# An encoder block on one core: filter spectra stored twice in DRAM, decay tiles loaded three ahead, the last hyena block loaded ahead

## The chip, the cores and the metric

The kernel runs on one core of one Trainium2 chip. The metric is the device time of one execution in microseconds (us). A core has TensorE (PE, matrix products and transposes through the systolic array into PSUM), VectorE (DVE), ScalarE (ACT) and GpSimd (POOL); SyncE (SP) issues nearly all the DMA transfers, which 16 DMA engines carry out.

## The reference, cut to what matters

One layer of a bidirectional encoder block, all in fp32, on 2048 positions and a model width of 1024. The projection to 2048 columns gives 512 columns for a Fourier mixing and 3 x 512 for a gated long convolution (hyena) of order two, whose filters are made by a small network and a decay.

```python
def implicit_filters(...):
    ...
    h = (h @ w_out).reshape(l, HYENA_ORDER, N_DIRECTIONS, HYENA_WIDTH)
    decay = jnp.exp(-t[:, None] * jnp.abs(deltas)[None, :])
    h = h * decay[:, None, None, :]
    ...
    return k * lax.rsqrt(jnp.sum(k * k, axis=0, keepdims=True) + EPS)

def fft_long_conv(u, k_freq, d):
    uf = jnp.fft.rfft(u, n=2 * l, axis=1)
    y = jnp.fft.irfft(uf * k_freq[None], n=2 * l, axis=1)[:, :l]
    return y + u * d

def hyena_mix(...):
    ...
    k_freq = jnp.fft.rfft(k, axis=0)
    z = v
    for n, gate in enumerate((x1, x2)):
        z = gate * fft_long_conv(z, k_freq[:, n], long_d[n])
    return z

def reference(...):
    h = rmsnorm(x, g_mix)
    p = h @ w_in                       # 512 Fourier columns, 3 x 512 hyena columns
    y_f = rmsnorm(fourier_mix(u_f), g_fourier)
    y_h = rmsnorm(hyena_mix(u_h, ...), g_hyena)
    x = x + concat(y_f, y_h) @ w_out
    x = x + relu(rmsnorm(x, g_mlp) @ w_fc1) ** 2 @ w_fc2
    return rmsnorm(x, g_final)
```

## The kernel before

The times below are those of the profiled execution. The kernel goes through these stages:

- `project` (0 to 410 us): x times the input weights in two passes; beside it tables are loaded (`tables`, the list `got`) and fc2's weights are combined. The gates x1, x2 and v go to DRAM (`gates`).
- `fourier` beside the first two filter units (410 to 473 us). The main loop takes a step of each in turn.
- the filter spectra (473 to 627 us), in `filters`: eight units, two orders n by four column tiles ct of 128 channels. A unit is made in three parts of eight steps: `generate(q)` (PE L529 into `pk`, DVE L533 `kt` = pk times the decay tile `dec`, ACT L181 `kh`, the fp32r upper part, and on DVE or POOL L182 `kl`, the rest; L543/544 add up squares), `stage1(c)` (three products L189 to L191, and DVE's transpose L443 into `Gk`) and `stage2(q)` (PE L597, ACT L600 into `ks`, and at every second q the store to `kd` in DRAM, called `spec`, L602). While unit i goes through stage1 (steps 0 to 7) and stage2 (8 to 15), unit i + 2 is generated, at the steps that the list `GENERATE` gives for i. `normalise` scales by the norm, `skip` adds long_d, `LAST` places unit 7's stage1.
- `hyena` (627 to 840 us): eight blocks, again n by ct. For each: `first` (PE L691, DVE L443 into G), `second(q)` (PE L698 into `pz`; ACT L701/702 `zs`; DVE L704 `y` = pz times ks; POOL L705 zs times ks; L706 adds them into y), `inverse(q)` three steps later (`LAG`, PE L714 into `pv`, ACT L715), `turn` (DVE L443) and `gate` (PE L727, DVE L728). `spectrum(q)` brings a tile ks of 512 KB by two transfers of 64 partitions each (L677), in four buffers.
- the tail of hyena (840 to 878 us): the first two tokens' Fourier rows (`yf`, L801/803, their norm L827, their transpose `pt_y` L810), the weights of w_out (`ost`, L792, split at L184/185), the last gates, and the Fourier half of the product `po` for these tokens.
- `project_out`, fc1 and fc2 (878 us to the end).

The order of the work on each engine is the order in which the code is written; SP takes its transfers in order too, and waits at each for its buffer. The long_d rows (`dk8`) are loaded inside `filters` (L505), behind the project stage's stores. A decay tile is loaded when the generate that uses it is written (two buffers, L170):

```python
if q % 2 == 0:
    self.dec = load(fp, "dec", [P, 8, 128], A["decay"][self.ct][:, 4 * q : 4 * q + 8, :], 2)
```

The table `f2` serves both the filters and hyena's second stage, `a2` the inverse; a2 is loaded into a pool of its own (2 MB, issued at 592 us).

Of the kernel before, what the change touches and what calls it, by code (L numbers as in the profile page):

```python
# [10 lines left out]
F32 = mybir.dt.float32  # L11
# [15 lines left out]
def _tables():  # L27
# [56 lines left out]
    A2[:, 0, 0] *= 0.5  # L84
    T["f2"] = F2.reshape(128, 32, 128).astype(f32)
# [42 lines left out]
P = 128  # L128
# [6 lines left out]
def hybrid_block(ctx: ExitStack, tc: tile.TileContext, A, out):  # L135
# [9 lines left out]
    kd = [[scratch(f"spec{i}{n}", [P, 32, 128]) for n in range(2)] for i in range(4)]  # L145
# [350 lines left out]
    def filters(ctx, fp, gp, zp, zzs, norms, emb, wo, e1k, f2):  # L496
# [10 lines left out]
        nc.tensor.transpose(p[:, 0:8], rows, ident[0:8, 0:8])  # L507
        nc.scalar.copy(longd, p[:, 0:8])

        class Unit:  # L510
# [3 lines left out]
            def generate(self, q):  # L514
# [9 lines left out]
                if q % 2 == 0:  # L524
                    self.dec = load(fp, "dec", [P, 8, 128], A["decay"][self.ct][:, 4 * q : 4 * q + 8, :], 2)
# [13 lines left out]
                if q == 0:  # L539
                    nc.scalar.square(self.acc, k4)  # L540
                else:
                    sq = fp.tile([P, 4, 128], F32, tag="sqr", name="sqr")
                    nc.scalar.square(sq, k4)  # L543
                    nc.gpsimd.tensor_add(self.acc, self.acc, sq)
# [49 lines left out]
            def stage2(self, q):  # L594
# [9 lines left out]
        units = [Unit(ct, n) for n in range(2) for ct in range(4)]  # L604
        for u in units[:2]:
# [9 lines left out]
        GENERATE = [(3, 5, 7, 7, 9, 11, 13, 15)] * 5 + [(7, 7, 8, 9, 10, 11, 12, 13)]  # L615

        LAST = ((), (), (), (), (), (0, 1, 2), (3, 4, 5), (6, 7))
        for i, u in enumerate(units):
            new = units[i + 1] if i < 7 else None

            def generate(step):
                for q in range(8 if i < 6 else 0):
                    if GENERATE[i][q] == step:
                        units[i + 2].generate(q)

            for c in range(8 if new else 0):
# [3 lines left out]
                generate(c)  # L630
            for q in range(8):
                u.stage2(q)
                if i == 6:
                    for c in LAST[q]:
                        new.stage1(c)
                if i and new and q == (0 if i == 6 else 1):
                    new.normalise()

                if new and q == (2, 5, 5, 5, 5, 5, 4)[i]:
                    new.skip()  # L640
                generate(8 + q)
                if q % 4 == 0 and i > 4:
                    ct = 2 * i - 11 + q // 4
                    if 0 <= ct < 4:
                        cs = slice(128 * ct, 128 * ct + 128)
                        if ct == 0:
                            zzs.append(zp.tile([P, NT, 512], F32, tag="zz", name="zz"))
                        nc.sync.dma_start(zzs[0][:, :, cs], gd[0][:, :, cs])
                j = 8 * i + q - 50
                if 0 <= j < 8:  # L650
                    units[j // 2].scale(2 * (j % 2), nc.gpsimd)
                    units[j // 2].scale(2 * (j % 2) + 1, nc.vector)


    def hyena(hp, wp, rp, zz, e1, b1, f2, a2, out_weights, out_ahead):
# [6 lines left out]
        class Block:  # L662
            def __init__(self, n, ct):
                self.n, self.ct = n, ct
                self.cs = slice(128 * ct, 128 * ct + 128)
                self.y, self.ahead = {}, None
# [5 lines left out]
            def spectrum(self, q):  # L672

                ks = hp.tile([P, 2, 4, 128], F32, tag="ks", name="ks", bufs=4)
# [19 lines left out]
            def second(self, q):  # L694
                ks = self.ahead if q == 0 and self.ahead else self.spectrum(q)
# [737 lines left out]
```

## Time and profile before

| what | value |
|---|---|
| runs before | 2334.44, 2330.9, 2318.71 us |
| median | 2330.9 us |
| profiled execution | 2326.34 us |
| its span in the profile | 2324.5 us |
| mean granted clock of TensorE | 0.988 of full speed |

The rows further down are of four views. A row of the windows view gives a stretch of the span in us (from:to, then its length), for each engine its busy time and in brackets its instructions, then the share of TensorE's full clock that was granted (PEclk), the mean busy share of the DMA engines and what they moved. PEld are weight loads beside PE's products. A row of the timeline gives the start of an instruction, its time, engine, line, operation, output<-inputs, shapes and count, and in square brackets the idle time of the engine before it with what ended it. For SPq, the DMA-issuing queue of SP, it is the issue, not the transfer. A row of the groups by line gives the count, the busy time in us, the mean of one in ns, and the idle time before them with what ended it.

### The profile page before, as it was taken

Reading aid. Unit: us, or ns where it says so; the run is one execution under the profiler, and the core shown is the slowest. Engines: PE = TensorE matmul, PEld = TensorE weight load, DVE = VectorE, ACT = ScalarE, POOL = GpSimd, SP = SyncE. Lnnn points to the kernel's source line nnn. Section 1 sums busy time; section 2 is a strip of 40 time slices with the busy share of each in tenths; the row PEclk is TensorE's granted clock in tenths of the full one; section 3 lists DMA queues with packets and bytes.
Section 4 is the critical chain, followed back from the end, with each engine's and each line's share of the span. In section 5 each row is a group of like instructions: output and inputs, shape, how many; then the busy total and the mean of one; then the engine's idle time right before and its main releaser. Section 6 shows DMA issues by size and latency. Waiting matters only on the chain.

```text
span 2324.5 us, 31068 instructions
## 1 busy us (share of the span) xinstructions
PE 2244.5 (97%) x11025; PEld 1859.5 (80%) x11025; DVE 1514.7 (65%) x2256; ACT 1108.8 (48%) x1842; POOL 827.4 (36%) x625
## 2 busy tenths in 40 slices
PE   7999999899999979998999999999999999999998
PEld 6887788698888758886788877888888888888886
DVE  6999676677677775457544456444366666866667
ACT  6555211465455554445555556555543333533334
POOL 3444332567366532116655556555400000000000
PEclk9999999999999999999999999999999999999999
DMA  7535986557689985667544455444479766866631
GB/s 253 182 136 197 330 303 244 189 194 240 223 194 204 206 235 163 186 177 233 162 152 153 151 205 193 150 150 150 160 283 361 241 191 193 291 207 191 198 119 73
DMA packets 294716, 468.42 MB, mean 202 GB/s; under 512 B 18389, under 2 KB 142623, under 8 KB 290209
## 3 DMA queue, kind: packets, MB, share of 16 engines
q1 hardware_dynamic: 288897, 452.04, 61.3%
q10 hardware_dynamic: 5664, 14.41, 1.8%
q8 instruction: 86, 1.41, 0.3%
q14 instruction: 69, 0.57, 0.1%
HBM read 312.54 MB, written 152.27 MB: 200 GB/s over the span
## 4 chain that ended last, share of the span: by engine, by line
PE 62%; DMA 4%; DVE 4%; ACT 2%; issue 1%; POOL 1%; SPq 1%; POOLq 0%; DVEq 0%; ACTq 0%
PE p1u L189 5%; PE p1u L191 5%; PE p1u L190 5%; PE p2u L191 5%; PE p2u L189 5%; PE p2u L190 5%; PE p2v L189 3%; PE p2v L191 2%; PE p2v L190 2%; PE p1v L189 2%; PE p1v L191 2%; PE p1v L190 2%; DMA ks<-spec 2%; PE po L190 2%; PE po L191 2%; PE po L189 2%
## 5 line engine op out<-in xcount | busy, mean ns | idle before, releaser
L181 ACT CAST qahm<-ra 128x1024 fp32r<-128x1024 f32 x110 | 115.9, 1053 | 345.8 <-PE p2u L190 172.7
L182 DVE TENSOR_TENSOR qalm<-ra,qahm 128x1024 fp32r<-128x1024 f32 x110 | 134.6, 1224 | 154.6 <-ACT qahm L181 151.8
L1208 POOL TENSOR_TENSOR acc<-acc,gfin 128x512 f32<-128x512 f32 x4 | 5.1, 1277 | 633.0 <-DMA out<-acc 625.8
L189 PE MATMUL pu<-wh,xh 128*128 128x512 f32 x512 | 204.2, 400 | 5.8 <-ACT wh L184 4.6
L190 PE MATMUL pu<-wl,xh 128*128 128x512 f32 x512 | 201.1, 393 | 3.3 <-DVE wl L185 3.3
L191 PE MATMUL pu<-wh,xl 128*128 128x512 f32 x512 | 200.9, 393 | 1.7 <-DVE xl L182 1.6
L190 PE MATMUL p2u<-qblm,qahm 128*128 128x512 f32 x504 | 196.2, 389 | 0.5 <-DVE qblm L182 0.5
L189 PE MATMUL p2u<-qbhm,qahm 128*128 128x512 f32 x504 | 196.0, 389 | 0.0
L191 PE MATMUL p2u<-qbhm,qalm 128*128 128x512 f32 x504 | 195.8, 389 | 0.0
L182 DVE TENSOR_TENSOR qblm<-rb,qbhm 128x1024 fp32r<-128x1024 f32 x110 | 134.0, 1218 | 1.9 <-ACT qbhm L181 1.9
L380 POOL TENSOR_TENSOR acc<-acc,cw 128x512 f32<-128x512 f32 x45 | 59.4, 1320 | 201.5 <-DVE acc L357 200.0
L181 ACT CAST ahm<-s 128x512 fp32r<-128x512 f32 x124 | 76.6, 620 | 95.2 <-PE p1v L190 54.6
L182 POOL TENSOR_TENSOR alm<-W,ahm 128x512 fp32r<-128x512 f32 x63 | 85.3, 1354 | 92.9 <-ACT ahm L181 92.9
L189 PEld LDWEIGHTS pu<-wh,xh 128*128 128x128 f32 x512 | 97.1, 190 | 26.4 <-ACT wh L184 5.0
L181 ACT CAST qbhm<-rb 128x1024 fp32r<-128x1024 f32 x110 | 115.4, 1049 | 5.2 <-DMA a1m<-c 3.4
L190 PEld LDWEIGHTS pu<-wl,xh 128*128 128x128 f32 x512 | 97.1, 190 | 24.2 <-DVE wl L185 3.8
L191 PEld LDWEIGHTS pu<-wh,xl 128*128 128x128 f32 x512 | 97.0, 189 | 23.1 <-DVE xl L182 2.5
L190 PEld LDWEIGHTS p2u<-qblm,qahm 128*128 128x128 f32 x504 | 94.6, 188 | 20.6 <-DVE qblm L182 1.0
L189 PEld LDWEIGHTS p2u<-qbhm,qahm 128*128 128x128 f32 x504 | 94.5, 188 | 20.2 <-ACT qbhm L181 0.4
L191 PEld LDWEIGHTS p2u<-qbhm,qalm 128*128 128x128 f32 x504 | 94.6, 188 | 19.8
L189 PE MATMUL p1u<-bm,ahm 128*128 128x512 f32 x252 | 100.2, 398 | 7.2 <-ACT ku L1071 6.3
L181 ACT CAST ahm<-W 128x512 fp32r<-128x512 f32 x94 | 57.6, 615 | 102.5 <-PE p1u L190 96.0
(387 smaller groups left out, 6449.2 us busy)
## 6 DMA issues: line engine op xcount, KB each, us to landing
W<-in_w_fc SPq DMA_DIRECT2D x66, 512.0 KB, 4.6
ks<-spec SPq DMA_DIRECT2D x128, 256.0 KB, 6.6
rb<-td SPq DMA_DIRECT2D x64, 512.0 KB, 4.2
ra<-a1m SPq DMA_DIRECT2D x56, 512.0 KB, 6.8
ra<-a0m SPq DMA_DIRECT2D x54, 512.0 KB, 10.6
rb<-in_w_fc SPq DMA_DIRECT2D x46, 512.0 KB, 4.5
f<-in_w_fc SPq DMA_DIRECT2D x16, 1024.0 KB, 6.8
td<-f SPq DMA_DIRECT2D x16, 1024.0 KB, 5.2
```

The lines of the kernel that those rows point to most:

```text
L181: nc.scalar.copy(hi, src)
L182: (eng or nc.vector).tensor_sub(lo, src, hi)
L189: nc.tensor.matmul(o, lhsT=lh, rhs=rh, start=start, stop=False, skip_group_check=more)
L190: nc.tensor.matmul(o, lhsT=lh, rhs=rl, start=False, stop=False, skip_group_check=more)
L191: nc.tensor.matmul(o, lhsT=ll, rhs=rh, start=False, stop=stop, skip_group_check=more)
L380: nc.gpsimd.tensor_add(m1, m1, cw[:, 3, :])
L1208: nc.gpsimd.tensor_mul(acc[i][:, c], acc[i][:, c], gfin[:, c])
```

## The change

- The long_d rows (`dk8`) are loaded in the project stage, and emb's tile moves to the pool `tp`.
- `decay(k)` loads the decay tiles, from the third unit on three ahead of their use, in four places (two `dec`, two in the pool of the x rows). `sqr` has two buffers.
- Spectra lie in DRAM twice, in a layout [2, 64, 2, 4096]: each store writes 128 x 2 x 1024 floats, 1 MB instead of 512 KB. For that the filters use a table `f2k` with permuted columns; hyena's own `f2` is loaded later into emb's tile (`tabs`), and a2 into the place of the filters' table. A spectrum is read by one transfer of 128 partitions, 512 KB.
- Hyena begins with the first four spectra of block 0, each followed by a quarter of a2.
- Unit 7's generates have other steps, partly in unit 6's stage1; zz is loaded and scaled by two tables, `LOAD` and `SCALE`.
- In the last block all spectra are asked for at q = 1 (q from 4 on in the room of W), then the Fourier rows, the first w_out rows and the gate rows; the tail's order of weights, gates, turns and products is another, the norms of the first two tokens' hyena rows come earlier (`norms`), and the pairs' places alternate between G and V.

```diff
-    kd = [[scratch(f"spec{i}{n}", [P, 32, 128]) for n in range(2)] for i in range(4)]
+    kd = [[scratch(f"spec{i}{n}", [2, 64, 2, 32 * 128]) for n in range(2)] for i in range(4)]
...
-        rows = fp.tile([8, 128], F32, tag="dk8", name="dk8")
-        for n in range(2):
-            nc.sync.dma_start(rows[4 * n : 4 * n + 4, :], A["long_d"].rearrange("a (c n) j -> n (a c) j", n=2)[n])
...
-                    self.dec = load(fp, "dec", [P, 8, 128], A["decay"][self.ct][:, 4 * q : 4 * q + 8, :], 2)
+                    k = 4 * units.index(self) + q // 2
+                    for j in (range(8, 12) if k == 8 else (k + 3,) if k > 8 else (k,)):
+                        decay(j)
+                    self.dec = decs.pop(k)
...
-                    nc.sync.dma_start(kd[self.ct][self.n][:, 4 * q - 4 : 4 * q + 4, :], self.ks)
+                    dst = kd[self.ct][self.n].rearrange("h p s x -> (p s) h x")[:, :, 512 * q - 512 : 512 * q + 512]
+                    nc.sync.dma_start(dst, self.ks.rearrange("p (h f) c -> p h (f c)", h=1).broadcast_to([P, 2, 1024]))
...
+                decs[k] = pl.tile([P, 8, 128], F32, tag=tag, name="dec", bufs=2)
+                nc.sync.dma_start(decs[k], A["decay"][u.ct][:, q : q + 8, :])
...
-        GENERATE = [(3, 5, 7, 7, 9, 11, 13, 15)] * 5 + [(7, 7, 8, 9, 10, 11, 12, 13)]
+        GENERATE = [(3, 5, 7, 7, 9, 11, 13, 15)] * 5 + [(7, 9, 11, 13, 15, 16, 17, 18)]
...
-                src = kd[self.ct][self.n][:, 4 * q : 4 * q + 4, :].rearrange("(s p) f c -> p s f c", s=2)
-                for hf in (slice(0, 64), slice(64, 128)):
-                    nc.sync.dma_start(ks[hf], src)
+                if self is blocks[7] and q > 3:
+                    if q == 4:
+                        self.room = rp.tile([P, 4, 2, 4, 128], F32, tag="W", name="ks4")
+                    ks = self.room[:, q - 4]
+                else:
+                    ks = hp.tile([P, 2, 4, 128], F32, tag="ks", name="ks", bufs=4)
+                src = kd[self.ct][self.n].rearrange("h p s x -> (h p) s x")[:, :, 512 * q : 512 * q + 512]
+                nc.sync.dma_start(ks.rearrange("p s f c -> p s (f c)"), src)
...
-                (nc.gpsimd if self is not blocks[7] and q in (0, 1, 2, 3) else nc.vector).tensor_add(y, y, zs)
+                (nc.gpsimd if q in ((0, 1) if self is blocks[7] else (0, 1, 2, 3)) else nc.vector).tensor_add(y, y, zs)
...
+        for k in range(4):
+            blocks[0].ahead[k] = blocks[0].spectrum(k)
+            nc.sync.dma_start(a2[:, 8 * k : 8 * k + 8], A["a2"][:, 8 * k : 8 * k + 8])
...
+                if i == 7:
+                    if q == 1:
+                        cur.ahead.update((k, cur.spectrum(k)) for k in range(2, 8))
+                    elif q == 2:
+                        ahead = work.ahead(hp, cur.y[2][:, 0, 0:1])
+                        next(ahead)
+                    elif q == 5:
+                        for k in range(4):
+                            work.load(hp, k)
+                    elif q == 6:
+                        cur.load()
...
-        old.load()
         for q in range(8 - LAG, 8):
             old.inverse(q)
-        ahead = out_ahead(hp)
-        next(ahead)
+        for k in range(0, 2):
+            work.weights(hp, k)
         for q in range(4):
             older.gate(q)
-            old.turn(2 * q)
-            old.turn(2 * q + 1)
-        next(ahead, None)
-        for k in range(0, 4):
-            out_weights(hp, k)
-        for q in range(4):
+        for k in range(2, 4):
+            work.weights(hp, k)
+        next(ahead)
+        for c in range(8):
+            old.turn(c)
+        for q in (0, 2):
+            next(ahead)
             old.gate(q)
-        next(ahead, None)
+            old.gate(q + 1)
+            if q == 0:
+                work.norms(hp)
         for k in range(4, 8):
-            out_weights(hp, k)
+            work.weights(hp, k)
...
-                n = "G" if k < 4 else "V"
+                n = "GVGV"[k // 2]
...
+            got.append(cpool.tile([8, 128], F32, tag="dk8", name="dk8"))
+            for n in range(2):
+                nc.sync.dma_start(got[-1][4 * n : 4 * n + 4, :], A["long_d"].rearrange("a (c n) j -> n (a c) j", n=2)[n])
```

The order of the instructions changes at these places. DVE at the start of the Fourier stage; Gf are its transposes, kt and kl belong to the first filter unit. Before:

```order
L182 TENSOR_TENSOR e1l<-e1k,e1h 128x128
L443 STREAM_TRANSPOSE Gf<-pf_3612 128x8x2x32
L533 TENSOR_TENSOR kt<-pk,dec 128x512
L536 COPY k_3638<-kt 1x128
L182 TENSOR_TENSOR kl<-kt,kh 128x4x8x16
L443 STREAM_TRANSPOSE Gf<-pf_3643 128x8x2x32
L443 STREAM_TRANSPOSE Gf<-pf_3646 128x8x2x32
L533 TENSOR_TENSOR kt<-pk,dec 128x512
```

and with the change:

```order
L185 TENSOR_TENSOR e1l<-e1k,e1h 128x128
L446 STREAM_TRANSPOSE Gf<-pf_3615 128x8x2x32
L446 STREAM_TRANSPOSE Gf<-pf_3643 128x8x2x32
L446 STREAM_TRANSPOSE Gf<-pf_3646 128x8x2x32
L536 TENSOR_TENSOR kt<-pk,dec 128x512 x2
L539 COPY k_3638<-kt 1x128
L185 TENSOR_TENSOR kl<-kt,kh 128x4x8x16
```

All three transposes stand ahead of the first kt now, where one did.

PE from unit 5's last first-stage products to unit 6's; L529 and L532 are a generate of unit 7, L597 and L600 a second-stage step of unit 5, L189 to L194 first-stage products. Before:

```order
L529 MATMUL pk<-wo,emb 128x128 x8
L597 MATMUL pk_5291<-Gk,f_2586 128x128 x4
L529 MATMUL pk<-wo,emb 128x128 x4
L597 MATMUL pk_5312<-Gk,f_2586 128x128 x4
L553 MATMUL psum_k<-ones,acc 128x1
L529 MATMUL pk<-wo,emb 128x128 x4
L597 MATMUL pk_5349<-Gk,f_2586 128x128 x4
L529 MATMUL pk<-wo,emb 128x128 x4
L597 MATMUL pk_5370<-Gk,f_2586 128x128 x4
L529 MATMUL pk<-wo,emb 128x128 x4
L597 MATMUL pk_5389<-Gk,f_2586 128x128 x4
L529 MATMUL pk<-wo,emb 128x128 x4
```

and with the change, from the second stage's end into unit 6's first stage:

```order
L532 MATMUL pk<-wo,emb 128x128 x4
L600 MATMUL pk_5392<-Gk,f_2589 128x128 x4
L600 MATMUL pk_5399<-Gk,f_2589 128x128 x4
L532 MATMUL pk<-wo,emb 128x128 x4
L192 MATMUL pk_5419<-kh,e1h 128x512
L193 MATMUL pk_5419<-kl,e1h 128x512
L194 MATMUL pk_5419<-kh,e1l 128x512
L532 MATMUL pk<-wo,emb 128x128 x4
L192 MATMUL pk_5437<-kh,e1h 128x512
L193 MATMUL pk_5437<-kl,e1h 128x512
L194 MATMUL pk_5437<-kh,e1l 128x512
L532 MATMUL pk<-wo,emb 128x128 x4
```

A generate stood beside each second-stage step; now it stands beside every second one, and the last three beside first-stage products of unit 6.

SP at the end of hyena; spec_67 is the last block's spectrum, xg its gate rows, yf the Fourier rows, ost the rows of w_out. Before:

```order
L670 DMA xg<-gates_59 128x16x128
L677 DMA ks<-spec_67 64x2x512 x8
L670 DMA xg<-gates_59 128x16x128
L801 DMA yf<-yfd 64x2x256
L803 DMA yf<-yfd 64x2x256
L801 DMA yf<-yfd 64x2x256
L803 DMA yf<-yfd 64x2x256
L792 DMA ost<-in_w_out 128x1024 x8
```

and with the change:

```order
L704 DMA ks<-spec_67 128x2x512
L704 DMA ks<-spec_65 128x2x512
L704 DMA ks<-spec_67 128x2x512 x3
L834 DMA ost<-in_w_out 128x1024 x2
L704 DMA ks_7326<-spec_67 128x2x512 x4
L853 DMA yf<-yfd 64x2x256
L855 DMA yf<-yfd 64x2x256
L853 DMA yf<-yfd 64x2x256
L855 DMA yf<-yfd 64x2x256
L834 DMA ost<-in_w_out 128x1024 x2
L692 DMA xg<-gates_59 128x16x128
L834 DMA ost<-in_w_out 128x1024 x4
```

The Fourier rows, half of the w_out rows and the last gate rows moved ahead, among the last block's spectra or right behind them.

## Rows read from the trace of the kernel before

**Rows 1.** Windows by stage, 400 to 425 and 573 to 2324 us, all engines.

```profile
core 0: us, PE busy (x) PEld busy (x) DVE busy (x) ACT busy (x) POOL busy (x), PEclk, DMA share, GB/s
...
400.00:425.00 25.00, 16.53 (x66) 12.13 (x65) 13.07 (x20) 2.69 (x7) 5.63 (x5) 0.80 0.71 244
...
573.00:630.00 57.00, 50.88 (x346) 45.74 (x345) 39.03 (x66) 26.12 (x52) 26.70 (x20) 0.94 0.70 238
630.00:807.00 177.00, 170.65 (x1190) 148.93 (x1188) 134.35 (x208) 98.76 (x171) 107.18 (x95) 1.00 0.89 202
807.00:840.00 33.00, 25.38 (x178) 21.02 (x180) 21.91 (x34) 16.64 (x30) 14.50 (x13) 0.95 0.96 217
840.00:878.00 38.00, 31.90 (x130) 20.48 (x127) 28.34 (x62) 23.16 (x43) 10.10 (x8) 0.87 0.74 227
878.00:2324.00 1446.00, 1419.45 (x6304) 1167.00 (x6302) 852.76 (x1180) 688.04 (x1081) 411.10 (x285) 0.99 0.58 190
```

**Rows 2.** Windows, the five stretches with a granted clock of about one half.

```profile
418.60:423.20 4.60, 4.56 (x12) 3.06 (x13) 1.08 (x3) 1.49 (x5) 0.00 (x0) 0.50 0.69 242
602.50:607.70 5.20, 5.17 (x24) 5.17 (x25) 1.35 (x7) 1.27 (x3) 0.00 (x0) 0.50 0.00 0
833.00:836.60 3.60, 3.08 (x15) 2.71 (x13) 2.33 (x5) 0.60 (x1) 2.54 (x3) 0.53 1.19 245
846.60:853.50 6.90, 6.29 (x18) 2.65 (x20) 6.90 (x12) 5.20 (x8) 0.00 (x0) 0.51 0.31 106
874.00:877.20 3.20, 3.20 (x11) 2.62 (x10) 1.38 (x2) 0.79 (x2) 0.83 (x1) 0.50 0.31 82
```

**Rows 3.** Timeline of PE at the start of the Fourier stage.

```profile
418.64 0.24 PE L507 MATMUL plongd<-ident,dk 8*128 8x8 f32 x1 [8.47 <-DMA dk<-in_long_d]
```

**Rows 4.** Timeline of SP's queue (SPq) at the same place.

```profile
416.51 0.61 SPq L505 DMA_DIRECT2D dk<-in_long_d  x2
417.24 0.35 SPq L170 DMA_DIRECT2D dec<-in_decay  x1
```

**Rows 5.** Timeline of DVE, the first kt.

```profile
421.48 0.69 DVE L533 TENSOR_TENSOR kt<-pk,dec 128x512 f32<-128x512 f32 x1 [4.89 <-DMA dec<-in_decay]
```

**Rows 6.** Windows, the stretch from that kt to the last Gf near it.

```profile
421.48:442.06 20.58, 20.58 (x94) 12.98 (x92) 18.03 (x28) 9.61 (x18) 11.45 (x10) 0.95 0.30 92
```

**Rows 7.** Timeline of PE, the second stages of units 5 and 6.

```profile
579.05 0.71 PE L597 MATMUL pk<-Gk,f 128*128 128x128 f32 x4 [1.46 <-DVE Gk L443]
...
602.53 0.80 PE L597 MATMUL pk<-Gk,f 128*128 128x128 f32 x2 [3.85 <-DVE Gk L443]
```

**Rows 8.** Groups by line on DVE, 471 to 628 us.

```profile
L443 DVE STREAM_TRANSPOSE Gk<-pk 128x512 f32<-128x512 f32 x58 | 39.0, 698 | 0.9 <-PE pk L191 0.9
L533 DVE TENSOR_TENSOR kt<-pk,dec 128x512 f32<-128x512 f32 x47 | 31.6, 675 | 8.3 <-PE pk L529 6.0 <-DMA dec<-in_decay 1.2 <-POOL kl L182 0.8
L182 DVE TENSOR_TENSOR kl<-kt,kh 128x512 fp32r<-128x512 f32 x23 | 21.8, 950 | 4.3 <-ACT kh L181 4.2
```

**Rows 9.** Windows: one unit, steady hyena, a stretch of fc2.

```profile
473.50:492.50 19.00, 19.00 (x144) 17.39 (x143) 13.61 (x24) 12.05 (x23) 13.90 (x13) 1.00 0.60 212
655.00:800.00 145.00, 140.65 (x978) 120.94 (x977) 112.99 (x176) 80.95 (x142) 89.18 (x79) 1.00 0.88 199
1700.00:1800.00 100.00, 99.46 (x436) 81.49 (x436) 68.11 (x78) 38.79 (x39) 0.00 (x0) 1.00 0.98 357
```

**Rows 10.** The tile ks in hyena, 640 to 830 us: its transfers.

```profile
DMA to landing us min/median/max: 3.9/6.6/10.0
```

**Rows 11.** Timeline of DVE in the last block.

```profile
830.49 0.69 DVE L704 TENSOR_TENSOR y<-pz,ks 128x512 f32<-128x512 f32 x1 [3.08 <-DMA ks<-spec]
```

**Rows 12.** Timeline of PE, last block and tail.

```profile
832.56 0.68 PE L714 MATMUL pv<-y,a 128*128 128x128 f32 x3 [2.98 <-DVE y L706]
...
846.67 0.90 PE L810 MATMUL pt_y<-ident,yf 128*128 128x128 f32 x3 [3.35 <-ACT yf L827]
...
872.92 0.55 PE L810 MATMUL pt_y<-turn,oyn 128*128 128x128 f32 x3 [1.94 <-ACT oyn L864]
```

More of the change, by code (lines that the diff above doesn't have):

```diff
@@ L493, in fourier, with filters @@
             yield
-    def filters(ctx, fp, gp, zp, zzs, norms, emb, wo, e1k, f2):
+    def filters(ctx, tp, fx, fp, gp, zp, zzs, norms, emb, wo, e1k, f2, dk8, tabs):
         e1h, e1l = (fp.tile([P, P], FR, tag=n, name=n) for n in ("e1h", "e1l"))
@@ L541, in generate @@
                 else:
-                    sq = fp.tile([P, 4, 128], F32, tag="sqr", name="sqr")
+                    sq = fp.tile([P, 4, 128], F32, tag="sqr", name="sqr", bufs=2)
                     nc.scalar.square(sq, k4)
@@ L601, in stage2, with decay @@
                 if q % 2:
-                    nc.sync.dma_start(kd[self.ct][self.n][:, 4 * q - 4 : 4 * q + 4, :], self.ks)
+                    dst = kd[self.ct][self.n].rearrange("h p s x -> (p s) h x")[:, :, 512 * q - 512 : 512 * q + 512]
+                    nc.sync.dma_start(dst, self.ks.rearrange("p (h f) c -> p h (f c)", h=1).broadcast_to([P, 2, 1024]))
         units = [Unit(ct, n) for n in range(2) for ct in range(4)]
+        decs = {}
+        def decay(k):
+            if k < 32:
+                u, q = units[k // 4], 8 * (k % 4)
+                pl, tag = (fx, "xt") if k >= 8 and k % 2 else (fp, "dec")
+                decs[k] = pl.tile([P, 8, 128], F32, tag=tag, name="dec", bufs=2)
+                nc.sync.dma_start(decs[k], A["decay"][u.ct][:, q : q + 8, :])
         for u in units[:2]:
@@ L619, in filters, with others @@
             new = units[i + 1] if i < 7 else None
[L621 to L624, printed above, removed]
+            def others(step):
+                for j in (i, i - 1):
+                    for q in range(8 if 0 <= j < 6 else 0):
+                        if 16 * j + GENERATE[j][q] == 16 * i + step:
+                            units[j + 2].generate(q)
+                if (i, step) == (6, 5):
+                    tabs.append(tp.tile([P, 32, P], F32, tag="emb", name="f2h"))
+                    for f in range(0, 32, 8):
+                        nc.sync.dma_start(tabs[0][:, f : f + 8], A["f2"][:, f : f + 8])
+                if (i, step) in LOAD:
+                    cs = slice(128 * LOAD[i, step], 128 * LOAD[i, step] + 128)
+                    if not zzs:
+                        zzs.append(zp.tile([P, NT, 512], F32, tag="zz", name="zz"))
+                    nc.sync.dma_start(zzs[0][:, :, cs], gd[0][:, :, cs])
+                if (i, step) in SCALE:
+                    j = SCALE[i, step]
+                    units[j // 2].scale(2 * (j % 2), nc.gpsimd)
+                    units[j // 2].scale(2 * (j % 2) + 1, nc.vector)
             for c in range(8 if new else 0):
@@ L629, in filters @@
                     new.normalise()
-                generate(c)
+                others(c)
             for q in range(8):
                 u.stage2(q)
+                if new and q == (2, 5, 5, 5, 5, 5, 4)[i]:
+                    new.skip()
                 if i == 6:
@@ L635, in filters, with hyena @@
                         new.stage1(c)
-                if i and new and q == (0 if i == 6 else 1):
+                if i and new and q == 1:
                     new.normalise()
[L639 to L655, printed above, removed]
+                others(8 + q)
+    def hyena(hp, wp, rp, zz, e1, b1, f2, a2, work):
         def big(nm):
@@ L694, in second @@
             def second(self, q):
-                ks = self.ahead if q == 0 and self.ahead else self.spectrum(q)
+                ks = self.ahead.pop(q) if q in self.ahead else self.spectrum(q)
                 p = pa("pz2")
@@ L812, in parts, with norms @@
             return yh, yl
+        def norms(self, hp):
+            for t in tokens[0:2]:
+                junk = hp.tile([P, 512], BF16, tag="yjunk", name="yjunk")
+                self.r[t] = rms(self.zz[:, t, :], 512, junk, "h")
         def multiply(self, p, parts, g, h):
@@ L863, in front @@
                 yh, yl = (op.tile([P, 4, P], FR, tag=n, name=n, bufs=4) for n in ("oyh", "oyl"))
-                nc.scalar.mul(yn, y, rms(y, 512, yn, "fh"[g]))
+                nc.scalar.mul(yn, y, work.r[t] if g and t in work.r else rms(y, 512, yn, "fh"[g]))
                 r.append(work.parts(yn, yh, yl, 0 if g else t))
@@ L1367, in hybrid_block @@
             with pool("hyena") as hp:
-                hyena(hp, wp, rp, zz, e1z, b1, f2, a2, work.weights, work.ahead)
+                hyena(hp, wp, rp, zz, e1z, b1, f2h[0], f2, work)
             tabs.close()
```

45 lines of the change are left out of this document (26 added, 19 removed).

## The prediction

> **What bounds the kernel now.** I read the stages first [rows 1]. TensorE (PE) is the bound: from 878 us on, which the change hardly touches, it is busy 1419.45 of 1446 us, and in each stage ahead of that it is the engine with the longest busy time. So the change can win only what PE loses before 878 us, by standing idle and by running at half clock. Idle, span less busy: 8.47 us in 400 to 425, 6.12 in 573 to 630, 6.35 in 630 to 807, 7.62 in 807 to 840, 6.10 in 840 to 878 [rows 1], 34.7 in all. The clock next [rows 2]: in five short stretches the granted clock is about half (1.2 instead of 2.4 GHz), each behind or among waits of PE; half of the busy time in each is lost: 2.3 + 2.6 + 1.4 + 3.1 + 1.6 = 11.0 us. The ceiling of the change is thus 45.7 us.
>
> What ends each wait is read from single rows. At 418.64 PE has stood 8.47 us for the long_d rows (dk) [rows 3], which SP issues at 416.51, behind the project stage's last stores, and the first decay tile (dec) only at 417.24 [rows 4]; DVE, too, stands 4.89 us until that tile lands [rows 5]. At 579.05 and 602.53 PE waits 1.46 and 3.85 us for DVE's transposes of Gk [rows 7]. In hyena the waits end with y, which needs the spectra (ks) from DRAM: the DMA engines are 88% busy there for only 199 GB/s [rows 9], a load lands after 3.9 to 10.0 us [rows 10], and in the last block DVE stands 3.08 us for ks, PE behind it 2.98 [rows 11, 12]. Behind it PE waits 3.35 us for yf and 1.94 for oyn, both from ACT [rows 12].
>
> **A, start of the Fourier stage.** dk8 is loaded in the project stage, so the wait of 8.47 us and 2.3 us of clock behind it go: 10.8 at most. What is late next is DVE. PE can fill the eight PSUM banks, but a bank of pk comes free only with its kt on DVE, and kt needs dec. The two dk issues ahead of dec on SP are gone, so dec takes their place at 416.51, 0.7 us earlier [rows 4]; with the same 4.24 us to landing (417.24 to 421.48) kt starts at about 420.8. Two of the Gf transposes that followed it stand ahead of it now, in DVE's idle time: 1.4 us. From 421.48 to 442.06 DVE is busy 18.03 of 20.58 [rows 6]; of the 2.55 idle, in which it waited for PE, I take 1.9 as filled, since PE is then ahead. Sum 0.7 + 1.4 + 1.9 = 4.0. Bounds: 2 (the earlier dec and the transposes alone) and 8 (PE's lead is never used up). I take 4: DVE is 88% busy in that row, so it ends the stretch, near 438 instead of 442.
>
> **B, decay loads three ahead, sqr in two buffers, dk and norms code.** The kt group shows 1.2 us of idle time behind dec in a whole stage, off PE's path [rows 8]. Nothing gained. SP carries these loads among the stores, which wait for ks from ACT; a unit of 19 us uses four decay tiles, so three ahead cover 14 us against a landing of about 4.2. If that cover is gone, a kt is late by one landing, 4 us: in the range.
>
> **C, GENERATE, last units.** Unit 7's eight generates moved from steps 7 to 13 of unit 5 to steps 7 to 18, the last three into unit 6's first stage. The waits in 573 to 630 are 6.12, with 2.6 of clock 8.7. In unit 5 DVE had a generate (kt, kl) with almost each Gk to turn; spread out, that wait (1.46) goes. Around unit 6's first stage DVE now has about four kt at 0.675, half of four kl at 0.95 (DVE has 23 kl for 47 kt, POOL the others) and eight Gk at 0.698 [rows 8]: 2.7 + 1.9 + 5.6 = 10.2, and some 0.9 until PE reads the last Gk. PE's own work in that time is twelve of the 24 groups of a unit, which takes it 19.00 us without a gap [rows 9]: 9.5. A wait of 11.1 - 9.5 = 1.6 stays of 3.85. Gain 1.46 + 2.25 + 1.3 (half the clock loss of 2.6) = 5.0. Bounds 2 (the clock still falls, the wait moves) and 7.
>
> A kl on DVE takes 950 ns on the mean, a kt of the same size, with one operand in PSUM, 675 [rows 8]. The Trainium skill, "SBUF — State Buffer", section "SBUF: two separate sides", says that a DVE operation with two SBUF inputs and a GpSimd operation that reads SBUF take a shared port pair in turn, the whole instruction long. The rows agree in direction (950 against 675). By the rule the more even mix of kl on both engines lengthens each kl on DVE; were each of the two longer by one more POOL operation's rest, estimated at 0.8, the wait at unit 6 would stay near 3.2, C would be 2.5 (no clock won) and the sum 23.5, inside the forecast's own case.
>
> **D, spectra twice in DRAM, one 128-partition load.** The stores grow from 512 KB to 1 MB. In a unit of 19 us the DMA engines are 60% busy for 212 GB/s [rows 9], 4.0 MB; four stores add 2.1. At 212/0.60 = 353 GB/s the 6.1 MB take 17.3 us of 19: hidden behind PE, barely. In hyena the loads have the same bytes in half the issues. There 199 GB/s at 0.88 is 226 GB/s full; the fc2 stretch, with 128-partition loads, 357 at 0.98, 364 [rows 9]. The same 199 GB/s would then hold the engines 55% instead of 88%, and the queue that makes 10.0 us of 6.6 goes. Of the 6.35 us idle in 630 to 807 I take 5 as gone; a2 (2 MB) now comes in with the first spectra while unit 7's last stores drain, up to 4 MB at 353 GB/s, 11.6 us against 8 until the first inverse, mostly begun earlier: minus 0.5. D is 4.5, bounds 1 and 6.4.
>
> **E, last block and tail.** E1: 807 to 840 holds 7.62 idle and 1.4 of clock, 9.0. Everything that block 7 reads is now asked for from its first steps on, ks 4 to 7 into room of their own, so only the chain PE, ACT (zs), POOL, DVE, PE of the last step stays, about 1: 8.0; bounds 5 (ACT's yf squares ahead of zs) and 9.0. E2: yf comes early, so 3.35 and part of 3.1 of clock could go, but in that stretch DVE is busy 6.90 of 6.90 and ACT 5.20 [rows 2], with weights, transposes and products that all stay: 2.0 (0 to 4). E3: the second token's wait, 1.94 with 1.6 of clock: the norms are computed earlier, 2.5 (0 to 3.5). The w_out loads in front of xg(7) on SP wait for ks tiles to come free; xg(7) is needed only at the last gates, some 15 us on: nothing.
>
> **Sum.** 4 + 5 + 4.5 + 8 + 2 + 2.5 = 26. The profiled execution took 2326.3 (span 2324.5 and 1.8 around it), so 2300.3; the median of the runs is 2330.9, and 26 less is 2305, which I predict.
>
> **The rivals.**
> Nearly the whole ceiling: PE runs through, no clock falls. For it: each wait has its own cause, and each cause is edited. Against: DVE is full at A and E2. Gain 34 to 44, with 39: 2292.
> Hidden anyway: DVE and ACT replace the DMAs as last releaser, above all at A, C and E2. For it: DVE's 18.03 of 20.58 and 6.90 of 6.90. A 2, C 2, D 3, E 5: 12, 2319. That GENERATE only moves the Gk wait, so that the change doesn't do there what it says, belongs here.
> Slower: the doubled stores make the spectra stage DMA-bound. Place: units 0 to 6, the stores on SP and the dec loads behind them; PE would stand at L532 for pk banks held by kt. At 353 GB/s it doesn't decide; the break-even with 26 us is 3.7 us more in each of seven units, 22.7 us for 6.1 MB, 269 GB/s. At 240 GB/s a unit takes 25.4: 45 lost, 26 won, 2350. For it: the hyena stretch has 226 full. Against: its form is gone, and the spectra stretch itself shows 353.
>
> **How the numbers follow.** Forecast (gain 18 to 34) 0.53; nearly all 0.15; hidden 0.24; slower rival 0.08. 1%, about what a measurement of this kernel can tell from no change, is 23.3 us. Of the forecast's 0.53 some 0.41 lie over 23.3: faster 0.41 + 0.15 = 0.56. Within: 0.12 + 0.24 and 0.03 of the rival, 0.39. Slower 0.05. Range 2290 (gain 41, near the ceiling) to 2324 (gain 7, between the low ends' sum of 10 and nothing).
>
> **What would show it.** A: no wait at plongd, DVE's first kt near 420.8, its last Gf of the stretch near 438. C: the rows at 579 gone, one near 2 before unit 6's second stage. D: DMA share near 0.55 in hyena, landings of ks below 7 us, hardly any PE wait for y. E: 25 us from block 7's start to its last inverse, a wait below 2 before pt_y, full clock behind 846. The prediction is wrong if the spectra stage (473 to 573) has PE waits that are not in the trace of before, or if DVE is gapless while PE waits in A or C.

## The result and the profile after

The kernel with the change takes 2307.18 us at the median of six runs (2304.21 to 2311.54), beside 2329.62 of before; the ratio is 0.9912 with a 95% interval of 0.9888 to 0.9935. A second set of six runs gave 2307.97 and 0.9914 (0.9894 to 0.9934). The prediction was 2305.

The windows by stage of the changed kernel answer to [rows 1]; columns as there:

```profile
400.00:425.00 25.00, 22.66 (x97) 15.65 (x96) 15.51 (x24) 3.85 (x10) 7.07 (x7) 0.96 0.77 259
...
573.00:630.00 57.00, 52.35 (x345) 47.04 (x344) 33.70 (x60) 22.69 (x46) 20.35 (x15) 0.94 0.93 322
630.00:807.00 177.00, 174.29 (x1242) 151.54 (x1241) 137.74 (x216) 106.71 (x183) 118.41 (x105) 1.00 0.77 236
807.00:840.00 33.00, 25.21 (x141) 18.48 (x140) 26.56 (x48) 20.35 (x37) 6.70 (x6) 0.84 0.66 198
840.00:878.00 38.00, 35.00 (x155) 26.07 (x156) 21.19 (x59) 18.33 (x42) 11.15 (x8) 0.96 0.66 187
```

PE's idle time in 400 to 425 fell from 8.47 to 2.34 us, in 630 to 807 from 6.35 to 2.71; 807 to 840 still has 7.79, now at a clock of 0.84. But the windows cut the program at other places now, since everything comes earlier. So the time is better followed by marks: the start of the same PE instruction in each trace, and the stretch between two of them. There are two traces of each kernel (the second ones are those of before_again and after_again, below):

| mark (PE) | before | before, again | after | after, again |
|---|---|---|---|---|
| last product of `project` | 408.92 | 408.39 | 408.80 | 410.78 |
| unit 0, second stage | 473.74 | 473.29 | 467.89 | 470.00 |
| unit 4, second stage | 557.44 | 557.01 | 551.59 | 553.71 |
| unit 7, second stage | 620.04 | 622.55 | 612.46 | 612.49 |
| block 0, first product | 627.30 | 629.81 | 619.72 | 619.75 |
| block 7, second stage | 807.96 | 809.44 | 796.20 | 797.09 |
| block 7, last inverse | 838.60 | 838.89 | 823.03 | 825.87 |
| first transpose of `hm` | 883.47 | 883.58 | 867.45 | 867.03 |
| end of the span | 2324.5 | 2324.0 | 2309.7 | 2309.6 |

These are the means of two traces, after against before, each with the term of the sum that stood for it:

- from `project`'s end to unit 0: 5.7 us won (A: 4);
- unit 0 to unit 4: nothing, 83.71 in both (the doubled stores: 0);
- unit 4 to unit 7: 4.2 (C: 5);
- block 0 to block 7: 3.2 (D: 4.5);
- within block 7: 2.2 (E1: 8);
- from there to hm: 2.0 (E2 and E3: 4.5);
- the rest, `project` and all from hm on, lost 2.8.

Together that is 14.6 us in the profiled executions, where the medians say 22. Both profiled executions of the changed kernel (2311.5, 2311.4 us) are the slowest of their six runs, and those of before (2326.3, 2325.8) lie below the median of their kernel. The granted clock of the two slowest runs is 0.987 and 0.989, that of the other ten 0.989 to 0.991. Which stretch makes the difference of 7 us no trace shows.

PE still waits at these places in the changed kernel, by its timeline (A, C, block 7 twice, tail):

```profile
421.74 0.70 PE L455 MATMUL pf<-uf,e1f 128*128 128x512 f32 x1 [2.31 <-DVE kt L536]
...
594.59 0.79 PE L600 MATMUL pk<-Gk,f 128*128 128x128 f32 x2 [3.03 <-DVE Gk L446]
...
819.84 0.58 PE L741 MATMUL pv<-y,f 128*128 128x128 f32 x1 [4.50 <-DVE y L733]
...
823.03 0.55 PE L741 MATMUL pv<-y,f 128*128 128x128 f32 x1 [1.11 <-ACT V L742]
...
859.38 0.66 PE L862 MATMUL pt_y<-turn,oyn 128*128 128x128 f32 x4 [2.22 <-ACT oyn L923]
```

The wait at plongd [rows 3] is gone. Of the two of [rows 7] the second is left, 3.03 us; the first is 0.83 in this trace and below 0.4 in the other. That of 2.98 in block 7 [rows 12] has become 4.50, with another cause, which SP, ACT and DVE show:

```profile
808.58 0.61 SPq L853 DMA_DIRECT2D yf<-yfd  x1
...
816.47 0.63 ACT L217 ACTIVATE yjunk<-yf 128x512 bf16<-128x512 f32 x1 [2.90 <-DMA yf<-yfd]
...
817.30 0.69 DVE L731 TENSOR_TENSOR y<-pz,ks 128x512 f32<-128x512 f32 x1
```

The Fourier rows are issued at 808.58, behind six spectra and two w_out rows, and ACT can start on the first of them 7.9 us later. ACT comes to their squares before the last zs and the V copies and stands 2.90 us; the last y and PE stand behind it. The next two rows are one unit of the spectra stage, as in [rows 9], and hyena:

```profile
473.50:492.50 19.00, 19.00 (x146) 17.91 (x145) 14.11 (x24) 11.41 (x23) 13.92 (x12) 1.00 0.88 306
640.00:790.00 150.00, 148.37 (x1054) 129.41 (x1053) 119.84 (x188) 89.26 (x153) 101.07 (x89) 1.00 0.76 227
```

The stores took the DMA engines' share in a unit from 0.60 to 0.88. The rate for a full share, GB/s divided by share, is 348 GB/s (353 before), and PE runs through.

One sentence ahead of the prediction has to be corrected here: the order on the engines and on SP is not that of the code. A scheduler sets it when the program is built. The runs long_late and long_fp show that the room of the tile, and not the line of code, sets the place of a load.

### The profile page after: what moved, and what is told of

The parts are those of the page before. It is cut to its first block, busy times and chain, and to the rows that moved or that the text cites. A ratio compares the mean times of both kernels' runs of the same rounds, so it can differ in the third digit from the quotient of the medians.

```text
span 2309.7 us, 31036 instructions
## 1 busy us (share of the span) xinstructions
PE 2245.3 (97%) x11025; PEld 1860.7 (81%) x11025; DVE 1512.3 (65%) x2254; ACT 1108.9 (48%) x1844; POOL 835.9 (36%) x627
## 4 chain that ended last, share of the span: by engine, by line
PE 88%; DVE 4%; DMA 3%; ACT 3%; issue 1%; POOL 1%; SPq 0%; ACTq 0%; DVEq 0%; POOLq 0%
PE p2u L193 5%; PE p2u L192 5%; PE p2u L194 5%; PE p1u L194 5%; PE p1u L192 5%; PE p1u L193 5%; PE pu L193 5%; PE pu L194 5%; PE pu L192 5%; PE pk L600 3%; PE p2v L192 3%; PE p2v L194 3%; PE p2v L193 3%; PE pk L532 2%; PE p1v L192 2%; PE p1v L194 2%
## 5 line engine op out<-in xcount | busy, mean ns | idle before, releaser
L194 PE MATMUL pu<-wh,xl 128*128 128x512 f32 x512 | 202.0, 395 | 0.0
L194 PE MATMUL p2u<-qbhm,qalm 128*128 128x512 f32 x504 | 195.8, 389 | 0.0
L383 POOL TENSOR_TENSOR acc<-acc,cw 128x512 f32<-128x512 f32 x45 | 59.4, 1320 | 201.0 <-DVE acc L360 199.5
L194 PEld LDWEIGHTS pu<-wh,xl 128*128 128x128 f32 x512 | 98.0, 191 | 21.3 <-DVE xl L185 0.5
L194 PEld LDWEIGHTS p2u<-qbhm,qalm 128*128 128x128 f32 x504 | 94.6, 188 | 19.8
```

Of the source, the lines that this page charges most:

```text
L194: nc.tensor.matmul(o, lhsT=ll, rhs=rh, start=False, stop=stop, skip_group_check=more)
L383: nc.gpsimd.tensor_add(m1, m1, cw[:, 3, :])
```

## The experiments

All are the changed kernel with one thing altered, or with a few that are named, and are compared with its 2307 to 2308. The ratios are to the kernel before.

**norms_later.** The rows are loaded at the same place; their norms are written behind the last inverses.

```diff
             for t in tokens[0:2]:
-                y = self.fourier_rows(t, hp, "yf", 2, late)
+                rows.append(self.fourier_rows(t, hp, "yf", 2, late))
+            yield
+            for y in rows:
...
         for q in range(8 - LAG, 8):
             old.inverse(q)
+        next(ahead)
```

> The changed kernel with one thing moved: ACT's squares and scalings of the two Fourier rows (yf) stand behind block 7's last inverses instead of in its middle; the rows are still loaded early. Theory: PE's new wait of 4.50 us for y and 1.11 for V in block 7 is ACT standing 2.90 us for yf ahead of zs and V, and the half clock behind it follows from that wait. Then both waits go to at most 1 us, block 7 ends some 4 to 5 us earlier, and the time is 4 to 7 us below the changed kernel's 2307 (2300 to 2303). Rival: the chain of the last step (ACT zs, POOL, DVE) and DVE's load bound block 7 anyway, or the norms only come due at pt_y: the wait moves there, and the time stays within 2 us of the changed kernel's.

Measured: 2306.51 us (ratio 0.9907, 0.9886 to 0.9927). This is the time that the rival forecast, and not the theory's 2300 to 2303. The wait of 4.50 became 1.17, but 3.72 us followed, behind DVE's v_f of the same norm. The scheduler had put the first square ahead of the last zs again, so the run did not take the theory's cause away; the next one does.

**norms_behind_yf, norms_again.** Two things are altered: the norms are tied behind the last zs on ACT and the last y on DVE, and the rows are issued ahead of the last six spectra.

```diff
+        with tc.issue_after(old.az.ins), tc.issue_after(old.dy.ins):
+            next(ahead)
...
                     if q == 1:
+                        ahead = work.ahead(hp, cur.y[0][:, 0, 0:1])
+                        next(ahead)
                         cur.ahead.update((k, cur.spectrum(k)) for k in range(2, 8))
```

> The changed kernel with the two Fourier rows' loads issued ahead of the last six spectra, and their squares on ACT and norms on DVE held behind block 7's last zs and y. Theory (PE's wait in block 7 is ACT, then DVE, standing for yf in order): no PE wait above 1.5 us between block 7's start and its last inverse, which ends 23 to 24 us after block 7's start (26.8 in the changed kernel), no half clock behind it; pt_m comes 4 to 6 us earlier in the trace, time 2300 to 2304. Rival (the last step's own chain is as long): still 25 us or more.

> norms_behind_yf again. Theory (its 3.2 us in block 7's trace reach the end): 1 to 4 us below after_again. Rival (they are given back in the tail or lost in the spread): within 1 us of it or above.

Measured: 2305.84 us (0.9899, 0.9876 to 0.9922), and 2304.55 (0.9899, 0.9879 to 0.9919) beside 2307.97 of the changed kernel on the same chip. PE in block 7 of norms_again:

```profile
815.81 1.13 PE L741 MATMUL pv<-y,f 128*128 128x128 f32 x8 [1.47 <-ACT V L742]
818.10 1.65 PE L741 MATMUL pv<-y,f 128*128 128x128 f32 x8 [1.16 <-DVE y L733]
820.58 2.05 PE L741 MATMUL pv<-y,f 128*128 128x128 f32 x8 [0.83 <-DVE v_f L219]
```

No wait of 4 us is left, the longest are 1.70 and 1.47. From block 0's first product to the last inverse it takes 200.3 and 201.3 us, the changed kernel 203.3 and 206.1. So ACT's standing for yf was the wait, worth about 4 us there; which of the two alterations does it the runs do not separate. The half clock behind it stayed, against the expectation: the last inverse still takes 2.05 us, one at full clock 1.05. Of the total it is some 3 us, less than the first of the two expectations and within the second; the runs of the two kernels on that chip overlap (2300.51 to 2307.74 against 2306.29 to 2311.38). It is the fastest version measured.

**long_late.** The load of long_d is written in `filters`, the tile stays where the change put it.

> The changed kernel with the long_d rows loaded in the filters again, ahead of the first decay tile. Theory (part A is worth what the two traces show, 5.8 us, because DVE and the first decay tile are late next): PE waits 8 to 9 us at plongd again, the wait of 2.31 us for kt is gone, and the filters' first second stage (467.89 in the changed kernel) comes 5 to 7 us later; time 2312 to 2314. Rival (the gain was DVE's order of transposes and kt, or the tile moves, not the early rows): PE's later steps are delayed by less than 3 us.

Measured: 2308.8 us (0.9915, 0.9892 to 0.9939), no wait at plongd. The load stands nearly where it does in the changed kernel: SP issues it at 48.0 us, right behind wo, in the changed kernel at 46.5, right ahead of it. The scheduler has brought it forward over some 370 us of the program. So the run tells nothing of part A, but that the line of code does not set the time of a load.

**long_fp.** The tile is in the filters' pool again, and its load with it.

```diff
-            got.append(cpool.tile([8, 128], F32, tag="dk8", name="dk8"))
+            got.append(None)
...
+        dk8 = fp.tile([8, 128], F32, tag="dk8", name="dk8")
```

> The changed kernel with the long_d rows' tile in the filters' pool again, as before: the room is free only when the project stage has ended, so the load stands behind the last stores on SP, ahead of the first decay tile. Theory (part A is 5.8 us, bounded by DVE): PE waits about 8.5 us at plongd, the later wait for kt (2.31) is gone, the filters' first second stage comes 5 to 7 us later than in the changed kernel, time 2312 to 2314. Rival (the gain came from DVE's new order of transposes and kt): the first second stage comes less than 3 us later.

Measured: 2314.68 us (0.9935, 0.9909 to 0.9961). The timeline of PE has the wait back:

```profile
418.01 0.24 PE L510 MATMUL plongd<-ident,dk 8*128 8x8 f32 x1 [8.75 <-DMA dk<-in_long_d]
```

Unit 0's second stage comes 6.8 us later behind the project stage's end, and the wait for kt is gone, as expected. Part A is the early rows, worth 6 to 7 us.

**half_reads, single_store.** half_reads takes each spectrum by two transfers of 64 partitions, one from each copy; single_store also stores it once.

```diff
-                nc.sync.dma_start(ks.rearrange("p s f c -> p s (f c)"), src)
+                for hf in (slice(0, 64), slice(64, 128)):
+                    nc.sync.dma_start(ks[hf].rearrange("p s f c -> p s (f c)"), src[hf])
```

> The changed kernel with each spectrum read by two transfers of 64 partitions, one from each copy in DRAM, instead of one of 128; stores doubled as in the changed kernel. Theory (part D is the form of the read): between block 0's start and block 7's, where PE needed 172.8 us before and 168.6 with the change, it needs 171 to 174, DMA share in 640 to 790 rises from 0.76 to above 0.85, time 2310 to 2313. Rival (D came from the order of the loads, a2 and the first spectra ahead): 168 to 169.5, the time unchanged within 2 us.

> The changed kernel with spectra stored once (512 KB a store) and read by two transfers of 64 partitions; all early loads of the change stay. Theory (the 128-partition form of the read carries hyena, and the doubled stores cost nothing that PE sees): the spectra stage takes as long as in the changed kernel (144.6 us from the first second stage to the last), its DMA share falls from 0.89 to about 0.65, and hyena is as slow as with half_reads (213.7 us from the first block's start to the last second stage, the changed kernel 192.8), or up to 4 us better, as 8 MB less are written just ahead of it: time 2316 to 2323. Rival (the slow hyena of half_reads was the doubled stores draining while a2 and spectra come in): hyena takes below 203 us and the time is below 2312.

Measured: 2322.01 us (0.9971, 0.9953 to 0.9988) and 2322.36 (0.9967, 0.9950 to 0.9984). Windows of half_reads, then of single_store (spectra stage, hyena):

```profile
640.00:790.00 150.00, 137.96 (x947) 120.05 (x948) 108.33 (x168) 80.38 (x139) 87.33 (x77) 0.98 0.87 200
```

```profile
500.00:570.00 70.00, 70.00 (x515) 63.92 (x514) 55.05 (x96) 43.23 (x87) 53.82 (x44) 1.00 0.66 218
640.00:790.00 150.00, 136.93 (x951) 120.04 (x952) 107.09 (x167) 80.59 (x140) 90.02 (x80) 0.98 0.84 196
```

PE is idle 12.0 and 13.1 us of these 150, 1.6 in the changed kernel; a full share of the DMA engines moves 230 and 233 GB/s, 299 with the 128-partition form, 226 before. So the form of the read is worth 14 to 15 us in the changed kernel, more than twice what half_reads was expected to lose, and more than D and E1 won together (5.4). One form has one transfer of 512 KB, the other two of 256 KB; whether the partitions or the number of transfers count the runs do not separate. From block 0's first product to block 7's second stage both runs take longer (193.8 and 193.5 us; no_ahead_single, which reads alike, 187.2) than the kernel before (180.7 and 179.6), which reads in the same form. In half_reads block 0 and 1, where a2 now comes in among the spectra, hold waits of 1.38, 1.77, 1.94 and 3.45 us between 641 and 665. That the change's own early loads cost this with the old form is argued from these waits; no run takes the loads back.

The two medians are equal, so with the loads three ahead the doubled stores cost nothing that the runs can tell. But the traces are not equal: from unit 4's second stage to unit 7's single_store takes 64.4 us, half_reads 59.4. The part on C below comes back to this.

The Trainium skill, "SBUF — State Buffer", section "Door 1: The DMA port swizzle (why `[64,N]` ≈ `[32,N]`)", says that 64 partitions reach half of the 16 ports. The direction agrees; here the ratio is 299 to 230, 1.3, in a mix that also has gate rows of 128 partitions and in which two such reads of 64 follow each other.

**gen_old.** `GENERATE`'s last row is that of before.

> The changed kernel with unit 7's generates at the steps of before (7, 7, 8 to 13). Theory (moving them won the 2.1 us that PE gained between the second stages of units 4 and 5, and nothing more, since the wait at unit 6 stayed 3.03): unit 5's second stage comes about 2 us later, the wait at unit 6 is 3 to 4, time 1 to 3 us above the changed kernel's. Rival (the step list keeps DVE even and the rest hangs on it): unit 6 waits above 5 us, or a wait below 1.5 there, in which case the new list made it no better.

Measured: 2310.56 us (0.9924, 0.9905 to 0.9944). PE's waits in units 5 to 7 are four others, of 1.72, 0.81, 1.83 and 2.19 us, and unit 7's second stage comes at 612.45 instead of 612.46. The theory expected unit 5's second stage 2 us later; it comes 161.8 us behind the project stage's end, in the changed kernel 162.3 and 161.5. The new steps changed the places of the waits, and nothing that a trace shows of their sum. The median is 2.6 to 3.4 us higher; the four runs (2308.98 to 2311.99) lie in the upper part of the changed kernel's twelve (2304.21 to 2311.54), so a small gain by the steps is not excluded.

**no_ahead, no_ahead_single.** Decay tiles in two places, each asked for at its own use; no_ahead_single also stores and reads spectra as single_store does.

```diff
-                    for j in (range(8, 12) if k == 8 else (k + 3,) if k > 8 else (k,)):
-                        decay(j)
+                    decay(k)
...
-                pl, tag = (fx, "xt") if k >= 8 and k % 2 else (fp, "dec")
-                decs[k] = pl.tile([P, 8, 128], F32, tag=tag, name="dec", bufs=2)
+                decs[k] = fp.tile([P, 8, 128], F32, tag="dec", name="dec", bufs=2)
```

> The changed kernel with decay tiles in two places only, each asked for at its own generate, as before. Theory (the 2.1 us that PE gained between the second stages of units 4 and 5 are a late decay tile, for which DVE stood 1.17 us at 560.87 before): unit 5's second stage comes 1.5 to 2.5 us later than in the changed kernel, with a wait of 1.2 to 1.7 ahead of it, and the doubled stores may add a further late tile elsewhere; time 1 to 4 us above the changed kernel's. Rival (sqr's second buffer or the scaling's new places won it): less than 0.7 us between units 4 and 5.

> no_ahead with spectra stored once and read by 64-partition transfers. In no_ahead SP has four decay loads behind four stores of 1 MB in each unit, and the time rose to 2344.5. Theory (the decay tiles are late because they queue behind the doubled stores on SP; with the store back at 512 KB the scheduler puts a decay load between the stores, as before): the spectra stage from the first second stage to the last takes 144 to 148 us again (184.9 in no_ahead, 144.6 in the changed kernel), hyena is that of single_store, time 2320 to 2327. Rival (two places for decay tiles are too few whatever is stored): the stage takes above 160 us and the time is above 2340.

Measured: 2344.51 us (1.0065, 1.0042 to 1.0088) for no_ahead, slower than before, and 2320.99 (0.9966, 0.9951 to 0.9981) for no_ahead_single. SP's queue in no_ahead, in the changed kernel, in no_ahead_single:

```profile
490.82 10.73 SPq L606 DMA_DIRECT2D spec<-ks  x4
501.64 14.49 SPq L616 DMA_DIRECT2D dec<-in_decay  x4
517.46 11.52 SPq L606 DMA_DIRECT2D spec<-ks  x4
```

```profile
491.88 6.29 SPq L607 DMA_DIRECT2D spec<-ks  x3
498.26 0.42 SPq L618 DMA_DIRECT2D dec<-in_decay  x1
501.00 0.36 SPq L607 DMA_DIRECT2D spec<-ks  x1
```

```profile
491.61 3.05 SPq L606 DMA_DIRECT2D spec<-ks  x2
495.40 0.33 SPq L616 DMA_DIRECT2D dec<-in_decay  x1
497.54 3.51 SPq L606 DMA_DIRECT2D spec<-ks  x2
```

With stores of 1 MB and two places all four decay loads of a unit queue behind all four stores, which wait for ks; with stores of 512 KB, or with loads three ahead, a decay load goes between them. (Why the scheduler makes these orders no run shows.) In no_ahead PE then stands for what lacks its kt, four times for 2 to 4 us and once for long:

```profile
500.00:570.00 70.00, 62.23 (x425) 56.91 (x424) 41.70 (x74) 33.24 (x66) 38.50 (x34) 0.90 0.68 231
```

```profile
627.33 0.59 PE L555 MATMUL psum_k<-ones,acc 128*128 128x1 f32 x2 [11.54 <-POOL acc L549]
```

From unit 0's second stage to unit 7's it is 178.5 us in no_ahead (the 184.9 on record counted to a later product of the last group), 144.6 in the changed kernel and 146.7 in no_ahead_single. So loading ahead is what the doubled stores need: without it the time is 37 us longer, and the DMA engines have room all the while (0.68). The expectation for no_ahead was 1 to 4 us, by the late decay tile between units 4 and 5 alone; it missed the size tenfold. By itself loading ahead gains nothing: no_ahead_single is as fast as single_store (2320.99, 2322.36).

**after_again, before_again.** Both kernels once more, unaltered.

> The changed kernel again, beside norms_again on one chip: 2305 to 2309, ratio to before 0.990 to 0.993; its trace shows which of the differences between single traces repeat (the waits of 2.31, 3.03, 4.50 and 2.22 us should).

> The kernel before, for a second trace: the waits of 8.47 (plongd), 1.46 and 3.85 (Gk), 2.98 (y), 3.35 (yf) and 1.94 (oyn) us should come again within 0.5 us, and the marks at which the units and blocks begin, counted from the project stage's end, within 2 us; the total may lie anywhere in 2319 to 2340.

Measured: 2307.97 us (0.9914, 0.9894 to 0.9934) and, in a single run, 2325.76. The changed kernel's waits came again with 2.20, 3.03, 5.56 and 1.89 us; those of before with 8.95, 2.06, 4.49, 1.16 (for 2.98; the waits of block 7 are spread over more steps), 3.14 and 1.46. Three of the six waits of before missed the 0.5 us that were expected, and two marks, counted from the project stage's end, lie 3.0 us apart, where 2 were. A difference below 3 us is thus not to be read from one trace.

## Why the prediction was right

The time came out, 2307.18 for 2305, and the gain with it, 22 us for 26. The way there was in part luck. In the traces the terms of the sum won 17.3 us instead of 26, and with the 2.8 that the rest lost 14.6, nearer to the rival "hidden anyway" (12) than to the forecast; the 7 us that bring the medians up to 22 belong to no stretch that a trace shows. A and D came by the mechanism that was forecast. C, E1 and E3 came out other than forecast, and B had a cost that the prediction did not see.

- A was 5.7 for 4, for the reason given: DVE and the first decay tile are late next. kt starts at 420.99 (forecast 420.8), and PE waits for it 2.31. From there DVE is busy 16.01 of 16.01 us (18.03 of 20.58 in [rows 6]) and ends its last Gf at 436.7 (forecast 438). long_fp shows the early rows as the cause.
- B, "Nothing gained", was right as a sum and wrong as a reason. "If that cover is gone, a kt is late by one landing, 4 us" failed: no_ahead lost 37. I had priced the landing, not the order on SP, where the loads stand behind stores that grew. The slower rival was priced by the DMA engines' rate, and there it was far away (348 GB/s against a break-even of 269); its real place was the queue, and the loads three ahead in the same change take it out.
- C was 4.2 for 5, but not by `GENERATE`: gen_old has the same marks. The first wait of [rows 7] goes with the place of one instruction on DVE, the scaling of zz. In both traces of before, in single_store and in no_ahead_single it stands among the eight transposes Gk of unit 5, and PE waits 1.46, 2.06, 2.83 and 2.83 us for them. In the changed kernel, and in each run of it that keeps the doubled stores and the loads ahead, the eight run through, and PE waits 1.25 us at most. These are DVE's rows of before, single_store and the changed kernel:

```profile
577.08 0.69 DVE L582 TENSOR_TENSOR zz<-zz,norms 128x512 f32<-128x512 f32 x1
...
571.53 0.71 DVE L585 TENSOR_TENSOR zz<-zz,norms 128x512 f32<-128x512 f32 x1 [1.42 <-DMA zz<-gates]
...
566.12 4.89 DVE L446 STREAM_TRANSPOSE Gk<-pk 128x512 f32<-128x512 f32 x8
```

single_store has the new `GENERATE`, the decay loads, sqr's second buffer and the new steps of the scalings, and yet needs 64.4 us from unit 4 to unit 7, no_ahead_single 63.0 (62.6 and 65.5 before, 60.9 and 58.8 in the changed kernel). So none of these edits wins C without the larger stores, with which the scheduler orders DVE otherwise; no term of the sum had that.

- The wait at unit 6 stayed at 3.03, where 1.6 was forecast. PE's own work from unit 6's first product to the wait is 8.5 us (583.06 to 591.56), eight first-stage groups and three generates, not twelve groups and 9.5. And "half of four kl" was wrong: the code of both kernels gives DVE every kl of unit 7 (`self is not units[7]`). DVE is without a gap while PE waits, which the prediction named as a sign of being wrong:

```profile
591.60:594.50 2.90, 0.00 (x0) 0.00 (x0) 2.90 (x6) 0.50 (x1) 2.18 (x2) 0.86 1.09 379
```

- The rule of the Trainium skill that was weighed against C ("SBUF — State Buffer", section "SBUF: two separate sides") does not show in the means: the kl on DVE take 1009 and 960 ns in the two traces of the changed kernel, 950 and 1005 before. It does show in single instructions. Of the 91 kl in the spectra stage of these four traces, the 23 that no POOL instruction overlaps by more than 0.1 us take 0.67 to 0.69 us; 47 take 0.93 to 1.86, and POOL overlaps each of these by 0.37 us or more. The first kl below runs between two instructions of POOL, the second beside those in the third row:

```profile
585.51 0.69 DVE L185 TENSOR_TENSOR kl<-kt,kh 128x512 fp32r<-128x512 f32 x1
...
589.15 1.17 DVE L185 TENSOR_TENSOR kl<-kt,kh 128x512 fp32r<-128x512 f32 x1
...
588.13 3.34 POOL L547 TENSOR_TENSOR acc<-acc,sqr 128x512 f32<-128x512 f32 x2 [0.69 <-ACT sqr L546]
```

So the 950 of [rows 8] is a mixture of two prices. (The prediction's sum for that case has a slip: a wait of 3.2 leaves C at 1.46 + 0.65 = 2.1, not 2.5.)

- D was 3.2 for 4.5. "the engines 55% instead of 88%" failed: the share is 0.76 at 227 GB/s, 299 for a full share and not the 364 of fc2. The queue was short enough all the same. half_reads shows the form of the read to be the cause.
- E1 failed in size: 2.2 for 8. The step was "so only the chain ... of the last step stays, about 1". The bound of 5 named ACT's yf squares ahead of zs, and that is what happened, with DVE and the V copies behind it, and cost more than the bound allowed. Where norms_behind_yf and norms_again take it away, block 7 takes 23.6 and 24.5 us from its second stage to its last inverse (30.6 and 29.5 before): 6 of the 8.
- E2 and E3 were 2.0 for 4.5. "E3: the second token's wait" named the wrong token. L923 makes oyn, which PE waits for, from the third token's Fourier rows, and the norms of the first two do not touch these. Their load is issued at 849.96, behind W, and the wait is 1.6 to 2.3 us in every run of the changed kernel and its variants. Loading these rows earlier was not tried. E2's loss of clock in [rows 2] moved with the new wait in block 7 to 807 to 840 (0.84).

## What to carry to other kernels

Follow single waits by marks, in more than one trace, and ask of each new early load who stands in order behind it: a row that lands 8 us after its issue stopped ACT, then DVE, then PE. When stores grow, look at what is queued behind them on the issuing engine before the bandwidth; loading ahead, which gains nothing by itself (2320.99 against 2322.36), can be what keeps a larger store free (2307.18 against 2344.51). The form of a read, one transfer of 128 partitions against two of 64, was worth 14 to 15 us, more than the new order of loads around it. And a total that comes out does not show that its terms did: add them up from the traces.

## What was not expected of the hardware

A full share of the DMA engines is not one rate. In this kernel it moved 226 to 233 GB/s with 64-partition reads of 2 KB rows, 299 with the 128-partition form of the same reads, 348 in the spectra stage with the doubled stores and 364 in fc2. A forecast of the share from another stage's rate was off by a third (0.55 against 0.76). And the same DVE instruction, kl, had two prices, 0.67 to 0.69 us with POOL idle and up to 1.86 with POOL at work beside it.
